# Local attention with the band mask added in the row-maximum operation of VectorE instead of in a product on TensorE

## The chip, the cores and the metric

The kernel runs on one core of one Trainium2 chip. The metric is the device time of one execution in microseconds (us); the lower the better. The core's engines are called here as in the profile: PE (TensorE, matrix products into PSUM) with PEld (its weight loads), DVE (VectorE), ACT (ScalarE), POOL (GpSimd) and SP (SyncE, which issues the DMAs).

## The reference

One layer of a diffusion backbone over 1024 latent tokens of width 1024, with 256 context tokens in front. A modulated RMSNorm feeds one input projection and from it three token mixers: local attention over a window (8 query heads, 2 key/value heads, head width 64), global attention, and a bidirectional recurrence (HGRN2). They are lifted, gated, merged and projected; a gated feed-forward block with a depthwise convolution follows. The part that the change touches is the local attention:

```
qpos = blk * BLOCK + arange(BLOCK)          # BLOCK = WINDOW = 128, 8 blocks
kpos = (blk - 1) * BLOCK + arange(3 * BLOCK)
valid = (|kpos - qpos| <= WINDOW) & (kpos >= 0) & (kpos < S)
s_loc = where(valid, q @ band(k).T * hd**-0.5, -1e30)
s_ctx = q @ ck.T * hd**-0.5                 # 256 context keys, no mask
p = softmax([s_ctx, s_loc, s_sink])         # one sink logit per head
o = p_ctx @ cv + p_loc @ band(v)
```

Each block of 128 queries thus sees the 256 context keys, and its own block of keys with the one before and the one after. In the block before, a key counts if its place is at or after the query's; in the block after, if it is at or before it. The own block has no mask. The first and last block of queries have no block before or after.

## The kernel before, in words

All products are made at near float32 precision from pairs of operands in the type float32r: a number is split into a high part and the rest (`KH` and `KL` for the keys, `ph` and `pl` for the probabilities), and the products of the parts are summed in PSUM. A query's two parts lie side by side in one operand `QT` (64 rows each), so that two products, with `KH` and with `KL`, give the scores.

The stages follow each other: modulation and context, the projections and the recurrence (to about 500 us), the token-major projections with RoPE, local attention (`br == 0`), global attention (`br == 1`), the merge, the feed-forward block. The order of the instructions on each engine comes from a planner: it takes the program in the order in which it is written, with priorities, and orders it by estimated costs. A helper `weave` sets the written order: it draws from several generators in proportion to their lengths.

In `attention`, an iteration `it` is one block of 128 queries (`tt`, 8 of them) and one key/value group (`g`, 2 of them, 4 heads each): 16 iterations. First `lead` loads all keys and values (`prep`: DMA, casts, transposes `kt`), prepares the queries of two iterations (`qprep`: DMA, split, transposes `pq`, cast `QT`) and makes the scores of iteration 0. Then each iteration weaves three things: the scores and softmax of iteration `it + 1` (`softmax_window`), the product with the values of iteration `it` (`values`), and products of the output gates as filler (`gate_unit`, tile `gz`, with weights loaded and split at lines 172 to 176 into `wr`, `wh`, `wl`).

In `softmax_window`, a head's scores `sa` are a row of 512 or 640 numbers for each of 128 queries, in one of two PSUM buffers of two banks (`mm2`, which the global attention and others also use). Lines 1387 and 1388 make the 256 context scores, 1390 and 1391 those of the band of keys (256 columns in the first and last block, 384 elsewhere). Line 1392 adds the mask: a product of the unit matrix `identr` with the needed columns of `trir`, three blocks of 128 columns that hold 0 or -1e30. Line 1395 takes the negated row maximum on DVE, line 1397 its minimum with the negated sink logit `nsnk`; line 1399 is the exponential on ACT, from PSUM into the tile `pw` (8 buffers), with the row sums as accumulated result. Lines 1404 to 1407 work out the sink's share and the reciprocal of the sum, and line 1409 scales `pw` on POOL. In `values`, line 1321 transposes `pw` (tile `pp`, four of 128x128), line 1325 casts it to `ph` on ACT, line 1326 subtracts to `pl` on DVE, and lines 1307 and 1308 multiply with the values (`po`).

The masks come as `tri`, three blocks of 128x128 in float32 (192 KB), by a DMA at line 1241 on SP's queue, ahead of the loads of the keys (line 1251), and are cast to `trir` on ACT at line 1243.

Of the kernel before, what the change touches and what calls it, by code (L numbers as in the profile page):

```python
# [9 lines left out]
F32 = mybir.dt.float32  # L10
F32R = mybir.dt.float32r
U32 = mybir.dt.uint32
AF = mybir.ActivationFunctionType
ALU = mybir.AluOpType
AX = mybir.AxisListType
# [3 lines left out]
P = 128  # L19
# [1209 lines left out]
def attention(tc, nc, ap_, br, ins, kv_d, q_d, y_d, mm2, bank, ident, identr, fill_gen, fill_steps):  # L1229
    V, A, G, T, SP = nc.vector, nc.scalar, nc.gpsimd, nc.tensor, nc.sync  # L1230

    def tl(shape, tag, nm, bufs=2, dt=F32):
        return ap_.tile(shape, dt, tag=tag, name=f"{tag}{br}_{nm}", bufs=bufs)

    NK = 10
    KH = tl([P, 2, NK * P], "KH", 0, 1, F32R)
    KL = tl([P, 2, NK * P], "KL", 0, 1, F32R)
    VHL = tl([P, NK, 2, 2, 64], "VHL", 0, 1, F32R)
    if br == 0:
        tri = tl([P, 3 * P], "tri", 0, 1, F32)  # L1240
        SP.dma_start(tri, ins["tri"])
        trir = tl([P, 3 * P], "trir", 0, 1, F32R)
        A.copy(trir, tri)
        snk = tl([P, 8], "snk", 0, 1)
        SP.dma_start(snk, ins["sink"].to_broadcast([P, 8]))
        nsnk = tl([P, 8], "nsnk", 0, 1)
        V.tensor_scalar(out=nsnk, in0=snk, scalar1=-1.0, scalar2=None, op0=ALU.mult)
# [43 lines left out]
    def scores(it):  # L1291
        tt, g = divmod(it, 2)
        QT = QTs.pop(it)
        if br == 0:
            yield from softmax_window(nc, tl, mm2, tt, g, f"{it}_", QT, KH, KL, trir, identr, snk, nsnk, res)
        else:
            yield from softmax_global(nc, tl, mm2, g, f"{it}_", QT, KH, KL, res, rs)

# [49 lines left out]
    res, rs = {}, {}  # L1348
    def lead():
        for k0 in range(0, NK, 2):  # L1350
            prep(k0)
            yield
        qprep(0)
        qprep(1)
        yield
        yield from scores(0)
# [14 lines left out]
    man.close()  # L1371


def softmax_window(nc, tl, mm2, tt, g, nm, QT, KH, KL, trir, identr, snk, nsnk, res):
    V, A, G, T = nc.vector, nc.scalar, nc.gpsimd, nc.tensor
    lo, hi = max(tt - 1, 0), min(tt + 1, LT - 1)
    kts = [0, 1] + [2 + b for b in range(lo, hi + 1)]
    nk = len(kts) * P
    w = nk - 256
    m0 = (lo - (tt - 1)) * P  # L1380
    Ps = []
    st = tl([P, 8, 4], "st", nm)
    ng, sm, sk = st[:, 0], st[:, 1], st[:, 2]
    for h in range(4):

        sc = mm2(f"sa{nm}{h}").rearrange("p a b -> p (a b)")[:, 256:256 + nk]
        T.matmul(sc[:, :256], QT[:, h], KH[:, g, :256], start=True, stop=False)
        T.matmul(sc[:, :256], QT[:, h], KL[:, g, :256], start=False, stop=True)
        k = (2 + lo) * P
        T.matmul(sc[:, 256:], QT[:, h], KH[:, g, k:k + w], start=True, stop=False)  # L1390
        T.matmul(sc[:, 256:], QT[:, h], KL[:, g, k:k + w], start=False, stop=False)
        T.matmul(sc[:, 256:], identr, trir[:, m0:m0 + w], start=False, stop=True)
        n1 = ng[:, h:h + 1]
        hs = g * 4 + h
        V.tensor_reduce(out=n1, in_=sc, axis=AX.X, op=ALU.max, negate=True)

        V.tensor_tensor(out=n1, in0=n1, in1=nsnk[:, hs:hs + 1], op=ALU.min)
        pw = tl([P, 640], "pw", f"{nm}{h}", 8)
        A.activation(pw[:, :nk], sc, AF.Exp, bias=n1, accum_out=sm[:, h:h + 1])
        Ps.append(pw)  # L1400
        if h % NB == NB - 1:
            b = slice(h - NB + 1, h + 1)
            bs = slice(hs - NB + 1, hs + 1)
            V.tensor_tensor(out=sk[:, b], in0=snk[:, bs], in1=ng[:, b], op=ALU.add)
            A.activation(sk[:, b], sk[:, b], AF.Exp)
            V.tensor_tensor(out=sm[:, b], in0=sm[:, b], in1=sk[:, b], op=ALU.add)
            V.reciprocal(sm[:, b], sm[:, b])
            for j in range(h - NB + 1, h + 1):
                G.tensor_scalar(out=Ps[j][:, :nk], in0=Ps[j][:, :nk], scalar1=sm[:, j:j + 1], scalar2=1.0,
                                op0=ALU.mult, op1=ALU.mult)  # L1410
        yield
    res[2 * tt + g] = ((lambda h, n: Ps[h][:, n * P:(n + 1) * P]), kts)
# [86 lines left out]
def _tile_w(w, nk, ncol):  # L1499

    K, N = w.shape
    return np.ascontiguousarray(w.reshape(nk, P, N // ncol, ncol).transpose(2, 1, 0, 3).reshape(N // ncol, P, nk * ncol))


def prepare(inputs):
    i = {k: np.asarray(v) for k, v in inputs.items()}
    f = np.float32
    r = {}
    r["xT"] = np.ascontiguousarray(i["x"][0].T)
    r["x"] = np.ascontiguousarray(i["x"][0])  # L1510
    r["ctxT"] = np.ascontiguousarray(i["ctx"][0].T)
    r["cc"] = np.ascontiguousarray(np.stack([i["c"][0], i["c_ctx"]], -1).reshape(KT, P, 2).transpose(1, 0, 2))
    wm = i["w_mod"][0]
    r["w_mod"] = wm
    r["w_mod01"] = np.ascontiguousarray(
        wm[:, :2 * D].reshape(KT, P, 2, KT, P).transpose(3, 1, 2, 0, 4).reshape(KT, P, 2 * KT * P))
    r["b_mod"] = np.ascontiguousarray(i["b_mod"][0].reshape(48, P).T)
    r["gains"] = np.ascontiguousarray(
        np.stack([i["norm_mix"][0], i["norm_ffn"][0], i["norm_final"]]).reshape(3, KT, P).transpose(2, 0, 1))
    r["lb"] = np.ascontiguousarray(np.stack([i["lb_fwd"][0], i["lb_bwd"][0]]).reshape(8, P).T)  # L1520
    r["gn"] = np.ascontiguousarray(i["gn_c"][0].reshape(P, 1))

    eo = np.concatenate([np.arange(0, 64, 2), np.arange(1, 64, 2)])
    r["qn"] = np.ascontiguousarray(i["qn_b"][0][eo].reshape(1, 64))
    r["kn"] = np.ascontiguousarray(i["kn_b"][0][eo].reshape(1, 64))
    r["sink"] = np.ascontiguousarray(i["sink_a"][0].reshape(1, 8))
    w = i["w_in"][0]
    sizes = (512, 128, 128, 512, 128, 128, 512, 512, 512, 512, 512, 3072)
    o = np.cumsum((0,) + sizes)
    seg = [w[:, o[j]:o[j + 1]] for j in range(12)]  # L1530
    pe = lambda m: m.reshape(D, -1, 64)[:, :, eo].reshape(D, -1)
    r["w_tm"] = np.ascontiguousarray(np.concatenate(
        [pe(seg[0]), pe(seg[1]), seg[2], pe(seg[3]), pe(seg[4]), seg[5]], 1)
        .reshape(2, 4, P, 6, 256).transpose(3, 0, 2, 1, 4).reshape(12, P, 1024))
    r["w_cm"] = _tile_w(np.concatenate([seg[6], seg[7], seg[8], seg[9], seg[10], seg[11]], 1), KT, P)
    r["w_branch"] = np.concatenate([_tile_w(i["w_branch"][0, n], 4, 256) for n in range(3)], 0)
    r["w_out"] = _tile_w(i["w_out"][0], KT, P)
    r["w_up"] = _tile_w(i["w_up"][0], KT, P)
    wd = i["w_down"][0]

    r["w_down"] = np.ascontiguousarray(
        wd.reshape(FT // 2, 2, P, 2, 512).transpose(3, 0, 2, 1, 4).reshape(FT, P, 1024))
    r["w_dlast"] = np.ascontiguousarray(
        wd.reshape(FT, P, KT, P)[:, :, 4:].transpose(2, 1, 0, 3).reshape(4, P, FT * P))
    r["conv"] = np.ascontiguousarray(
        np.concatenate([i["w_dw"][0], i["b_dw"]], 0).reshape(4, 2 * FT, P).transpose(2, 1, 0))

    r["ident"] = np.eye(P, dtype=f)
    j, t = np.meshgrid(np.arange(P) % HB, np.arange(HB), indexing="ij")
    r["hmask"] = np.ascontiguousarray(  # L1550
        np.stack([((j >> l) ^ 1) == (t >> l) for l in range(NMASK)], 1).astype(np.uint32))
    q, k = np.meshgrid(np.arange(P), np.arange(P), indexing="ij")
    z = np.zeros((P, P))
    r["tri"] = np.concatenate([np.where(k >= q, z, -1e30), z, np.where(k <= q, z, -1e30)], 1).astype(f)
    row = np.repeat(np.arange(L // 64), 64).astype(f)
    col = np.tile(np.arange(64), L // 64).astype(f)
    inv = (f(10000.0) ** (-np.arange(0, 32, 2, dtype=f) / f(32))).astype(f)
    ang = np.concatenate([row[:, None] * inv, col[:, None] * inv], -1).astype(f)
    cs = np.stack([np.cos(ang), np.sin(ang)], 1).astype(f)
    r["rope"] = np.ascontiguousarray(cs.reshape(LT, P, 2, 32).transpose(1, 0, 2, 3))  # L1560
    return r
# [15 lines left out]
```

## Time and profile before

| what | value |
|---|---|
| time, median of 3 runs | 2128.88 us (2126.53 to 2129.55) |
| span of the profiled execution | 2127.9 us |
| instructions | 30555 |
| PE busy | 2085.8 us (98%), 11686 matmuls |
| PE weight loads busy | 1743.1 us (82%) |
| DVE busy | 1380.5 us (65%) |
| ACT busy | 1001.2 us (47%) |
| POOL busy | 288.1 us (14%) |
| DMA | 229.28 MB, 108 GB/s on average |
| local attention, first to last `sa` product | 699.6 to 877.1 us |

The page gives the span from the first to the last instruction as the profiled execution's only time; the median of the runs lies 1.0 us above it. Busy times are those of the profiled execution. PE's are sums over matmuls whose ends are modelled, and neighbours overlap, so a matmul's share of the time is read from the distance of starts. In the lists of groups, a row gives the line, the engine, the operation, what is written from what, the count, then the sum and the mean (ns) of busy time, and then the idle time before it with the one that ended it.

### The profile page before, as it was taken

What the parts mean: (1) busy time and instruction counts of PE and PEld (TensorE: products, weight loads), DVE (VectorE), ACT (ScalarE), POOL (GpSimd) and SP (SyncE); (2) the same over time, 40 slices, a digit from 0 to 9 for tenths busy, and PEclk for the clock granted to TensorE, in tenths of its full rate; (3) what the DMA queues carried; (4) which work ended last, traced back from release to release, by engine and by line L of the source; (5) the groups of instructions that cost most, each with busy time, mean ns of one, the idle gap of its engine ahead of it and who ended that gap; (6) DMA issues with size and microseconds to landing.
All of it is one profiled execution on the core that took longest, in us unless ns stands there. A gap on an engine that the chain in (4) does not pass through costs nothing.

```text
span 2127.9 us, 30555 instructions
## 1 busy us (share of the span) xinstructions
PE 2085.8 (98%) x11686; PEld 1743.1 (82%) x11686; DVE 1380.5 (65%) x2299; ACT 1001.2 (47%) x1761; POOL 288.1 (14%) x257
## 2 busy tenths in 40 slices
PE   7999999999999999999999999999999999999997
PEld 4888888888988888878888788888888888888887
DVE  4736756636665777678887746569777777664423
ACT  4333333311123777678888734346445544453222
POOL 0000000010021222100000000011333344100111
PEclk9999999999999999999999999999999999999999
DMA  9511111136543211211100354641222222285342
GB/s 359 207 44 36 46 50 41 46 113 214 186 137 123 78 59 41 80 55 35 35 28 28 115 200 142 194 156 55 99 79 89 80 80 88 81 287 201 109 126 86
DMA packets 95490, 229.28 MB, mean 108 GB/s; under 512 B 10736, under 2 KB 35824, under 8 KB 94320
## 3 DMA queue, kind: packets, MB, share of 16 engines
q1 hardware_dynamic: 95344, 227.33, 32.1%
q8 instruction: 92, 1.51, 0.3%
q14 instruction: 54, 0.44, 0.1%
HBM read 181.68 MB, written 45.61 MB: 107 GB/s over the span
## 4 chain that ended last, share of the span: by engine, by line
PE 69%; DVE 3%; ACT 2%; issue 1%; DMA 1%; POOL 1%; SPq 0%; DVEq 0%; ACTq 0%; POOLq 0%
PE pp L1321 4%; PE gz L199 3%; PE dn L929 3%; PE dn L928 3%; PE dn L930 3%; PE gz L200 3%; PE gz L201 3%; PE up L852 2%; PE up L853 2%; PE up L854 2%; PE po L1307 2%; PE po L1308 2%; PE br L200 2%; PE br L201 2%; PE br L199 2%; PE upd L853 2%
## 5 line engine op out<-in xcount | busy, mean ns | idle before, releaser
L175 ACT CAST wh<-wr 128x1024 fp32r<-128x1024 f32 (+1 forms) x139 | 145.1, 1044 | 398.7 <-PE dn L929 69.1
L176 DVE TENSOR_TENSOR wl<-wr,wh 128x1024 fp32r<-128x1024 f32 (+1 forms) x139 | 171.1, 1232 | 221.1 <-ACT wh L175 206.7
L1326 DVE TENSOR_TENSOR pl<-pp,ph 128x512 fp32r<-128x512 f32 x236 | 159.3, 687 | 29.2 <-ACT ph L1325 23.5
L199 PE MATMUL gz<-hh,wh 128*128 128x512 f32 x384 | 156.3, 408 | 3.1 <-ACT gs L523 3.1
L1325 ACT CAST ph<-pp 128x512 fp32r<-128x512 f32 x236 | 135.7, 587 | 37.4 <-PE pp L1321 35.3
L201 PE MATMUL gz<-hh,wl 128*128 128x512 f32 x384 | 152.3, 397 | 0.0
L200 PE MATMUL gz<-hl,wh 128*128 128x512 f32 x384 | 152.1, 396 | 0.0
L210 PE MATMUL tm<-wl,hh 128*128 128x256 f32 x384 | 108.9, 283 | 3.3 <-DVE wl L176 3.3
L209 PE MATMUL tm<-wh,hh 128*128 128x256 f32 x384 | 108.9, 284 | 0.9 <-ACT qo L615 0.9
L211 PE MATMUL tm<-wh,hl 128*128 128x256 f32 x384 | 108.6, 283 | 0.0
L1307 PE MATMUL po<-ph,VHL 128*128 128x512 f32 x236 | 106.1, 450 | 1.4 <-ACT ph L1325 1.0
L929 PE MATMUL dn<-ac,wh 128*128 128x512 f32 x256 | 99.7, 390 | 0.0
L930 PE MATMUL dn<-ac,wl 128*128 128x512 f32 x256 | 99.6, 389 | 0.0
L928 PE MATMUL dn<-ac,wh 128*128 128x512 f32 x256 | 99.6, 390 | 0.0
L1308 PE MATMUL po<-pl,VHL 128*128 128x512 f32 x236 | 97.1, 411 | 0.1
L199 PEld LDWEIGHTS gz<-hh,wh 128*128 128x128 f32 x384 | 72.7, 189 | 17.2 <-ACT gs L523 5.2
L201 PEld LDWEIGHTS gz<-hh,wl 128*128 128x128 f32 x384 | 72.5, 189 | 15.0
L200 PEld LDWEIGHTS gz<-hl,wh 128*128 128x128 f32 x384 | 72.8, 190 | 11.6
L210 PEld LDWEIGHTS tm<-wl,hh 128*128 128x128 f32 x384 | 73.7, 192 | 4.3 <-DVE wl L176 4.0
L1321 PE MATMUL pp<-ident,plat 128*128 128x128 f32 x512 | 76.6, 273 | 0.0
L1321 PEld LDWEIGHTS pp<-ident,plat 128*128 128x128 f32 x512 | 62.7, 140 | 16.9 <-DVE pl L1326 1.2
L199 PE MATMUL br<-yh,wh 128*128 128x512 f32 x192 | 74.3, 390 | 1.6 <-ACT yh L1468 1.6
(1420 smaller groups left out, 5898.7 us busy)
## 6 DMA issues: line engine op xcount, KB each, us to landing
wr<-in_w_cm SPq DMA_DIRECT2D x48, 512.0 KB, 3.7
wr<-in_w_up SPq DMA_DIRECT2D x44, 512.0 KB, 3.5
wr<-in_w_down SPq DMA_DIRECT2D x33, 512.0 KB, 3.5
wmr<-in_w_mod SPq DMA_DIRECT2D x32, 512.0 KB, 4.5
gate_d<-gs SPq DMA_DIRECT2D x48, 256.0 KB, 2.3
sgt<-gate_d SPq DMA_DIRECT2D x24, 512.0 KB, 3.4
act_d<-u SPq DMA_DIRECT2D x22, 512.0 KB, 2.6
st<-act_d SPq DMA_DIRECT2D x44, 256.0 KB, 4.5
```

The costliest lines, as they stand in the source:

```text
L175: A.copy(hi[:, :n], raw[:, :n])
L176: (lo_eng or V).tensor_tensor(out=lo[:, :n], in0=raw[:, :n], in1=hi[:, :n].bitcast(F32), op=ALU.subtract)
L199: T.matmul(psl, wh[:, k, c], hh[:, k0 + k, cols], start=s, stop=False)
L200: T.matmul(psl, wh[:, k, c], hl[:, k0 + k, cols], start=False, stop=False)
L201: T.matmul(psl, wl[:, k, c], hh[:, k0 + k, cols], start=False, stop=e)
L210: T.matmul(psl, hh[:, k, toks], wl[:, k % 4, :], start=False, stop=False)
L928: T.matmul(z, w[0][:, c], h[0], start=s, stop=False)
L929: T.matmul(z, w[0][:, c], h[1], start=False, stop=False)
L930: T.matmul(z, w[1][:, c], h[0], start=False, stop=e)
L1307: T.matmul(po, vv, ph, start=n == 0, stop=False)
L1321: T.transpose(pp[:, h], PT(h, n), ident)
L1326: V.tensor_tensor(out=pl, in0=pp, in1=ph.bitcast(F32), op=ALU.subtract)
```

## The change

The mask product on PE goes. In place of the reduction and the minimum on DVE, one DVE operation adds the scores in PSUM and a band of masks in SBUF, multiplies by -1, writes the row to `pw`, and gives the minimum of that row and `nsnk`. The exponential then works in place on `pw` in SBUF, with scale -1. The band holds nine blocks of 128 columns, of which 640 columns from the first on serve the inner and the last block of queries (the last takes 512 of them), and the last 512 the first block; the context keys have zeros in it. It stays in float32, and the cast of the masks goes.

```diff
     if br == 0:
-        tri = tl([P, 3 * P], "tri", 0, 1, F32)
-        SP.dma_start(tri, ins["tri"])
-        trir = tl([P, 3 * P], "trir", 0, 1, F32R)
-        A.copy(trir, tri)
+        band = tl([P, 9 * P], "band", 0, 1, F32)
+        SP.dma_start(band, ins["band"])
...
-    m0 = (lo - (tt - 1)) * P
+    m0 = 0 if tt else 5 * P
...
-        T.matmul(sc[:, 256:], QT[:, h], KL[:, g, k:k + w], start=False, stop=False)
-        T.matmul(sc[:, 256:], identr, trir[:, m0:m0 + w], start=False, stop=True)
+        T.matmul(sc[:, 256:], QT[:, h], KL[:, g, k:k + w], start=False, stop=True)
         n1 = ng[:, h:h + 1]
         hs = g * 4 + h
-        V.tensor_reduce(out=n1, in_=sc, axis=AX.X, op=ALU.max, negate=True)
-
-        V.tensor_tensor(out=n1, in0=n1, in1=nsnk[:, hs:hs + 1], op=ALU.min)
         pw = tl([P, 640], "pw", f"{nm}{h}", 8)
-        A.activation(pw[:, :nk], sc, AF.Exp, bias=n1, accum_out=sm[:, h:h + 1])
+        V.tensor_tensor_reduce(out=pw[:, :nk], in0=sc, in1=band[:, m0:m0 + nk], scale=-1.0, scalar=nsnk[:, hs:hs + 1],
+                               op0=ALU.add, op1=ALU.min, accum_out=n1)
+        A.activation(pw[:, :nk], pw[:, :nk], AF.Exp, bias=n1, scale=-1.0, accum_out=sm[:, h:h + 1])
...
-    r["tri"] = np.concatenate([np.where(k >= q, z, -1e30), z, np.where(k <= q, z, -1e30)], 1).astype(f)
+    bl, br = np.where(k >= q, z, -1e30), np.where(k <= q, z, -1e30)
+    r["band"] = np.concatenate([z, z, bl, z, br, z, z, z, br], 1).astype(f)
```

More of the change, by code (lines that the diff above doesn't have):

```diff
@@ L1294, in scores @@
         if br == 0:
-            yield from softmax_window(nc, tl, mm2, tt, g, f"{it}_", QT, KH, KL, trir, identr, snk, nsnk, res)
+            yield from softmax_window(nc, tl, mm2, tt, g, f"{it}_", QT, KH, KL, band, snk, nsnk, res)
         else:
@@ L1371, in attention, with softmax_window @@
     man.close()
-def softmax_window(nc, tl, mm2, tt, g, nm, QT, KH, KL, trir, identr, snk, nsnk, res):
+def softmax_window(nc, tl, mm2, tt, g, nm, QT, KH, KL, band, snk, nsnk, res):
     V, A, G, T = nc.vector, nc.scalar, nc.gpsimd, nc.tensor
```

## The prediction

> **What bounds the kernel now.** I read the busy time by stretch first, cut where local attention lies.
>
> ```profile
> core 0: us, PE busy (x) PEld busy (x) DVE busy (x) ACT busy (x) POOL busy (x), PEclk, DMA share, GB/s
> 690.00:880.00 190.00, 188.44 (x1124) 161.62 (x1123) 146.78 (x450) 140.06 (x357) 48.95 (x64) 1.00 0.19 56
> 0.00:2128.00 2128.00, 2085.81 (x11686) 1743.08 (x11686) 1380.50 (x2299) 1001.23 (x1761) 288.14 (x257) 1.00 0.32 108
> ```
>
> The columns are the stretch, its length, then each engine's busy time. PE is busy 188.4 of 190 us in the stage of local attention, and 2085.8 of 2128 in all; DVE stands at 77% of the stage and ACT at 74%. The clock is 1.00, so no throttle has to be reckoned with. A busy PE could still hide stalls inside its modelled durations, so the second view is the waits of PE and of its weight loads in the stage:
>
> ```profile
> PE pp L1321 <- ACT QT L1288: 0.7, 4, 0.2
> ...
> PEld pp L1321 <- ACT QT L1288: 1.6, 4, 0.4
> PEld pp L1321 <- POOL pw L1409: 1.1, 4, 0.3
> ```
>
> The columns are the total, the times and the longest. The largest wait of PE is 0.7 us in 190, and its weight loads lose at most 1.6 us to any one releaser. The third view is the chain that ended last, cut to the stage:
>
> ```profile
> by line: PE pp L1321 16.5%; PE gz L199 11.0%; PE gz L200 10.8%; PE gz L201 10.2%; PE po L1307 7.9%; PE po L1308 7.9%; PE sa L1391 5.0%; PE sa L1390 5.0%; PE sa L1392 5.0%; PE sa L1387 3.9%; PE sa L1388 3.4%; ACT pw L1399 2.3%; PE pq L1286 1
> ```
>
> The mask product, line 1392, is 5.0% of 190 us of this chain, 9.5 us. So it lies on the path that sets the end, and TensorE's issue of instructions is the limit here. After the stage nothing waits for a fixed moment: the next stage is again PE work, and what ends earlier here starts earlier there.
>
> **The change part by part.** *The mask product removed (64 times, with its weight load).* Its duration in the rows, about 0.34 us, is not what it costs, since matmuls overlap. What counts is the distance between starts, from the timeline of PE:
>
> ```profile
> 753.49 0.34 PE L1390 MATMUL sa<-KH,QT 128*128 128x384 f32 x1
> 753.66 0.34 PE L1391 MATMUL sa<-KL,QT 128*128 128x384 f32 x1
> 753.84 0.34 PE L1392 MATMUL sa<-trir,identr 128*128 128x384 f32 x1
> 754.02 0.60 PE L1321 MATMUL pp<-ident,pw 128*128 128x128 f32 x4
> ...
> 873.15 0.28 PE L1392 MATMUL sa<-trir,identr 128*128 128x256 f32 x1
> 873.26 0.60 PE L1321 MATMUL pp<-ident,pw 128*128 128x128 f32 x4
> ```
>
> Three products over 384 columns take 754.02 - 753.49 = 0.53 us, 0.177 each; one over 256 takes 873.26 - 873.15 = 0.11. There are 48 of the wide form (the twelve (tile, group) pairs inside the sequence, four heads each) and 16 of the narrow one (the first and the last tile): 48 x 0.177 + 16 x 0.11 = 10.3 us. The chain says 9.5. These are the bounds; I take 10.0 us saved, between two readings of the same thing.
>
> *The DVE work.* The reduction and the small minimum go, one fused operation comes that reads the scores from PSUM and the band from SBUF, writes the whole masked row to `pw`, and gives the row minimum. The trace has no such operation; the nearest rows:
>
> ```profile
> L1395 DVE TENSOR_REDUCE st__6601<-sa 128x1 f32<-128x640 f32 x4 | 3.3, 822 | 2.3 <-PE pp L1321 1.2 <-PE sa L1392 1.1
> L1395 DVE TENSOR_REDUCE st__6194<-sa 128x1 f32<-128x512 f32 x4 | 2.7, 686 | 0.9 <-PE sa L1392 0.9
> L1326 DVE TENSOR_TENSOR pl<-pp,ph 128x512 fp32r<-128x512 f32 x72 | 49.0, 686 | 6.0 <-ACT ph L1325 5.3
> L1282 DVE SCALAR_TENSOR_TENSOR qs_q<-qf_q,qs_q 128x256 fp32r<-128x256 f32 x16 | 6.7, 418 | 4.0 <-PE sa L1392 2.2 <-ACT qs_q L1281 1.8
> 690.00:880.00 190.00, 9.89 (x64) 1.00 0.19 56
> 690.00:880.00 190.00, 50.30 (x64) 1.00 0.19 56
> ```
>
> The last two rows are the busy time of line 1397 and of line 1395 alone. `pl` has the new operation's operands (one from PSUM, one from SBUF, a full row out) and costs 686 ns for 512 elements, the same as the reduction. So the likely price is that of the reduction, 50.3 us for 64, and 9.9 us of line 1397 go: DVE 146.8 - 9.9 = 136.9 us. The low end is this; for the high end the operation runs at half the rate. The rows at 640 and 512 give (822 - 686) / 128 = 1.06 ns per element, so half rate adds 0.68 us at 640 and 0.54 at 512: 48 x 0.68 + 16 x 0.54 = 41 us, DVE 178 us. An accumulated result may need a read-out besides; ACT's costs
>
> ```profile
> L1399 ACT ACTIVATE pw<-sa,st__6457 x4: 795/800/813, 721.3 to 726.6; 128x640 f32<-128x640 f32 x4
> L1399 ACT ACTIVATION_READ_ACCUMULATOR pw<-sa,st__6457 x4: 193/197/212, 722.0 to 727.3; 128x1 f32 x4
> L1399 ACT ACTIVATE pw<-sa,st__6194 x4: 677/682/688, 703.4 to 708.3; 128x512 f32<-128x512 f32 x4
> L1443 ACT ACTIVATE pc__8872<-pc__8872,st__8871 x4: 495/498/518, 916.8 to 923.3; 128x256 f32<-128x256 f32 x4
> ```
>
> 0.2 us, so 0 to 64 x 0.2 = 13 us. I take full rate with a small read-out, DVE about 143 us beside a PE that needs 178 to 180. It is hidden by PE. The fused operation waits for the products as the reduction did, with the same work queued behind it on DVE. One wait is new to DVE: as the writer of `pw` it now waits for the transposes that last read that buffer, which ACT did before. With eight buffers these belong to the iteration before last, all issued before this one's scores, so I count nothing for it.
>
> The row that bears on half rate is line 1282: two float32 sources, both in SBUF, 256 elements in 418 ns. At 1.06 ns per element that is 271 ns and a fixed 147, so full rate, though that operation has no accumulator. [...]
>
> *The exponential* reads `pw` in SBUF instead of PSUM. From PSUM, 512 and 640 elements take 682 and 800 ns, 0.92 ns per element, so 256 would take 0.446; line 1443, in place in SBUF, takes 0.498. So +0.05 us each, 3.3 us on ACT (74% busy before). It frees the score buffer earlier, after the DVE operation; the stage waits almost nothing for that now, so I count nothing.
>
> *Where ACT's cover is thin.* At four boundaries between iterations the chain leaves PE for ACT's queue:
>
> ```profile
> 739.89 0.41 ACT wh L175
> ...
> 740.84 0.88 ACT pw L1399 x2
> ...
> 743.09 0.59 ACT QT L1288
> 743.73 0.55 PE pp L1321 x3
> ```
>
> The weight cast, an exponential, a gate copy, two copies of `ytmp` and the cast of `QT` run back to back from 739.9 to 743.7, and the transposes behind need `QT`; PE waited there, the 0.7 us in four times above. This burst doesn't shrink, while PE's work beside it loses one or two mask products, 0.18 to 0.35 us, and the exponential in it grows by 0.05. So some 0.3 us at each of four places are not gained: +1.2 us; bounds 0 and 4 x 0.7 (four products of an iteration) = 2.8.
>
> *The masks' load.* `band` is 9 blocks of 64 KB, 576 KB, where `tri` had 192; the cast `trir` goes.
>
> ```profile
> L1241 SPq DMA_DIRECT2D tri<-in_tri x1: 447/447/447, 678.8 to 678.8; - x1
> DMA to landing us min/median/max: 3.8/3.8/3.8
> ...
> 682.66 0.51 ACT L1243 CAST trir<-tri 128x384 fp32r<-128x384 f32 x1 [0.29 <-DMA tri<-in_tri]
> ...
> 685.18 0.54 PE L1270 MATMUL kt<-identr,qs_kk 128*128 128x128 f32 x4 [0.26 <-ACT qs_kk L1261]
> ...
> wr<-in_w_cm SPq DMA_DIRECT2D x48, 512.0 KB, 3.7
> ```
>
> A 512 KB load lands in 3.7 us against 3.8 for `tri`, so the size alone hardly shows, but the first keys are issued behind it on the same queue, and PE waits for them (0.26 us at 685.18). The price lies between -0.3 (that wait gone with ACT's cast) and 384 KB at the 512 / 3.7 = 138 KB per us of that load, +2.8 us, all at once. I take +0.5. The band itself has time: the first exponential, at 703.4, comes 20 us after the old cast.
>
> *Sum.* -10.0 + 1.2 + 0.5 = -8.3 us against the profiled span of 2127.9, so 2119.6. The median of the runs, 2128.88, is 1.0 us above that span, so 2120.6 us.
>
> **The rivals.** *The order eats it (no change).* The order on the engines is planned anew with other durations. Each of 16 iterations has only to lose 0.6 us more on PE for 10 us to go. For it: ACT's bursts above, and the scaling on POOL, for which weight loads already wait 1.1 us in four places and which now has a DVE beside it that writes full rows. Against it: DVE and ACT are idle a quarter of the stage and PE hardly waits. Time: 2128.9 - 10 + 16 x (0.4 to 0.7) = 2125 to 2130, say 2127.
>
> *The fused operation is slow (slower).* One mechanism: half rate on DVE. DVE then needs 178 us of work and up to 13 of read-outs, 178 to 191, in a stage where PE needs 188.4 - 10.0 = 178.4. DVE would be the bound. PE, kept in order by its own queue, is idle for 2% of the span; for DVE, fed by two engines, I assume 5%, and the stage takes 187 to 201 us instead of 190: 2126 to 2140, say 2135 with a read-out. It decides where DVE's work reaches about 180 us, that is at (180 - 86.6) / 64 = 1.46 us for each fused operation (86.6 is 146.8 without lines 1395 and 1397); below about 1.2 us nothing shows. For it: no row has this operation. Against it: lines 1326 and 1282.
>
> *The gain is larger.* The earlier release of the score buffers and a better fit of the new order take ACT's waits away: the full 10.3 us plus the 3.4 us that the rows of waits show, 2115.5.
>
> **How the numbers follow.** Forecast, 2116.5 to 2124.5: 0.57. Larger gain: 0.11. Order eats it: 0.18. Slow operation: 0.10. Some other loss in the new order beyond 0.2%: 0.04. About 0.2%, 4.3 us, is what this measurement can tell from no change; the edge of the faster class is 2124.6. Faster: 0.57 + 0.11 and a small part of the order rival's, 0.70. Same: 0.16. Slower: 0.14. The range reaches from the larger gain, with a bit of room, 2114, through the whole of the order rival, 2130; the slow operation lies outside.
>
> **What would show it.** Right: line 1392 gone from PE with 64 fewer products; the fused operation at about 0.82 to 0.95 us for 640 elements; the stage from the first `sa` product to the last some 8 to 10 us shorter with PE still above 97% busy; the exponential at 0.84 to 0.85 us. Wrong: a fused operation above 1.2 us with PE waiting for ACT's exponential or POOL's scaling behind it; PE's idle time in the stage above 8 us; or a start of local attention delayed by over 2 us, with the keys' load as its cause.

## The result, and the profile after

The changed kernel takes 2119.15 us (median of 4 runs, 2117.39 to 2122.27) against 2127.70 us for the kernel before in the same series (2126.43 to 2129.55). The ratio is 0.9959, 95% interval 0.9944 to 0.9973: faster by 8.6 us, where 8.3 had been forecast. A repeat with another series of the kernel before gave 2119.38 against 2129.49 us, ratio 0.9956 (0.9943 to 0.9970).

The profile of the changed kernel, first the busy times of its engines over the whole, then the stage of local attention by stretch (columns as before; the stage is cut at 872 us, since it ends earlier):

```profile
PE 2078.3 (98%) x11622; PEld 1735.2 (82%) x11622; DVE 1379.4 (65%) x2299; ACT 1003.0 (47%) x1760; POOL 289.7 (14%) x257
...
690.00:872.00 182.00, 178.94 (x1062) 150.98 (x1061) 144.52 (x451) 143.35 (x360) 49.83 (x64) 1.00 0.19 60
```

There are 64 matmuls fewer (11622 for 11686) and one ACT cast fewer. DVE's count stays at 2299, since the 64 minima that went are replaced by 64 read-outs of an accumulator.

The groups of the changed kernel by shape, for the fused operation and for the exponential:

```profile
L1393 DVE CUSTOM_DVE_ANT_0 pw<-sa,band,nsnk 128x640 f32<-128x640 f32 x48 | 42.2, 880 | 5.5 <-PE sa L1389 4.9
...
L1393 DVE CUSTOM_DVE_ANT_0 pw<-sa,band,nsnk 128x512 f32<-128x512 f32 x16 | 11.9, 747 | 2.9 <-PE sa L1389 1.9 <-PE pp L1319 0.8
...
L1395 ACT ACTIVATE pw<-pw,st__8062 128x640 f32<-128x640 f32 x4 | 3.3, 834 | 0.0
```

The fused operation takes 880 ns for 640 elements, 58 ns more than the reduction took, and 1.04 ns per element from one shape to the other, where the reduction took 1.06: the reduction's rate, which the prediction calls full. The exponential from SBUF takes 0.83 us where it took 0.80. In the timeline of DVE the read-out is a row of its own, and the next operation starts with it:

```profile
729.12 0.88 DVE L1393 CUSTOM_DVE_ANT_0 pw<-sa,band,nsnk 128x640 f32<-128x640 f32 x1
729.93 0.08 DVE L1393 DVE_READ_ACCUMULATOR2_ANT st__6575<- 128x1 f32 x1
729.93 0.69 DVE L1324 TENSOR_TENSOR pl<-pp,ph 128x512 fp32r<-128x512 f32 x1
```

So the read-out costs the queue nothing here (the subtraction starts at 729.93 as well). The waits of PE and of its weight loads in the stage:

```profile
PE pp L1319 <- POOL pw L1405: 1.5, 5, 0.6
PE pq L1284 <- DVE qs_q L1280: 1.4, 1, 1.4
...
PEld pp L1319 <- POOL pw L1405: 3.5, 8, 0.9
...
PEld pp L1319 <- ACT QT L1286: 1.6, 4, 0.4
```

The weight loads' wait for `QT` is what it was, 1.6 us; PE's own, 0.7 us before, is not in the list any more. New is the wait of the transposes `pp` for the scaling on POOL, 3.5 us of the loads where it was 1.1 and 1.5 us of PE, and the wait for the second queries (`pq`) grew from 0.5 to 1.4 us.

**A cleaner measure than the time.** Executions of one kernel differ by several microseconds (the four of the changed kernel by 4.9), and part of this lies ahead of the change (5.4 us between two executions of the same work, in the last section). So the experiments are read by a stretch as well, from the start of the last token-major product (`tm`) to the first key transpose of the global attention (`kt`). It holds all of local attention, and the same PE work in every kernel but for what the experiment takes out. Before:

```profile
663.90:894.56 230.66, 227.61 (x1313) 193.00 (x1312) 167.05 (x495) 156.47 (x390) 51.65 (x66) 1.00 0.23 72
```

The changed kernel:

```profile
663.70:885.96 222.26, 217.87 (x1250) 182.46 (x1249) 164.71 (x495) 158.60 (x389) 51.84 (x66) 1.00 0.24 76
```

The stretch is 8.4 us shorter, and PE's busy time in it falls by 9.7 us. The repeat of the changed kernel:

```profile
664.00:884.60 220.60, 217.64 (x1249) 182.37 (x1248) 164.50 (x495) 158.22 (x389) 51.51 (x66) 1.00 0.25 77
```

There the stretch was 220.6 us, 10.1 shorter, so differences under 2 us in it aren't read. Of every other kernel one execution was profiled. What follows the stretch takes 1231.6 us after and 1233.3 before, much the same: the gain is made in this stage.

### The profile page after: what moved, and what is told of

The parts are those of the page before. It is cut to its first block, busy times and chain, and to the rows that moved or that the text cites. A ratio compares the mean times of both kernels' runs of the same rounds, so it can differ in the third digit from the quotient of the medians.

```text
span 2117.6 us, 30402 instructions
## 1 busy us (share of the span) xinstructions
PE 2078.3 (98%) x11622; PEld 1735.2 (82%) x11622; DVE 1379.4 (65%) x2299; ACT 1003.0 (47%) x1760; POOL 289.7 (14%) x257
## 4 chain that ended last, share of the span: by engine, by line
PE 69%; DVE 3%; ACT 2%; issue 1%; POOL 1%; DMA 1%; DVEq 0%; ACTq 0%; POOLq 0%; SPq 0%
PE pp L1319 5%; PE gz L199 3%; PE gz L200 3%; PE gz L201 3%; PE dn L929 3%; PE dn L930 3%; PE dn L928 3%; PE up L852 2%; PE up L853 2%; PE up L854 2%; PE po L1305 2%; PE po L1306 2%; PE br L200 2%; PE br L201 2%; PE br L199 2%; PE upc L854 2%
## 5 line engine op out<-in xcount | busy, mean ns | idle before, releaser
L733 ACT ACTIVATE u<-c,cw 128x1024 f32<-128x1024 f32 x38 | 47.3, 1246 | 61.9 <-DVE c L889 33.1
```

## The experiments

The theory ahead of the runs was that the 64 slots taken from PE are the gain. The rival was that the gain comes from the other half of the change, a shorter path on DVE and score buffers that are freed earlier.

**The product alone removed.**

```diff
-        T.matmul(sc[:, 256:], QT[:, h], KL[:, g, k:k + w], start=False, stop=False)
-        T.matmul(sc[:, 256:], identr, trir[:, m0:m0 + w], start=False, stop=True)
+        T.matmul(sc[:, 256:], QT[:, h], KL[:, g, k:k + w], start=False, stop=True)
```

(on the kernel before)

> The kernel before with the mask product alone taken from PE; reduction, minimum and exponential stay as they were, and the mask is left out of the computation. Theory (the gain is the 64 slots of the product on PE): 9.5 to 10.3 us less than before, less up to 1.2 us at ACT's bursts, so a ratio of 0.9952 to 0.9960 and a time some 0 to 1.5 us below the changed kernel's, which pays for the longer load. Rival (the gain comes from the one DVE operation in place of two and the score buffer freed earlier): a ratio of 0.9985 to 1.000.

Measured: 2123.49 us against 2128.91, ratio 0.9977 (0.9968 to 0.9986). By this time it fits neither. The nine runs had a higher clock than the 27 of before, though, 0.9976 against 0.9964 in the mean. With each run's span multiplied by its granted clock, the 5.4 us become 2.9, as an estimate, which is the rival's edge. The stretch, at a clock of 1.00 like before's, says the same:

```profile
660.30:888.20 227.90, 221.45 (x1250) 180.68 (x1249) 172.62 (x495) 155.46 (x390) 51.97 (x66) 1.00 0.23 73
```

It is only 2.8 us shorter than before. The waits of this kernel, in a window around local attention, show where the slots went:

```profile
PE pp L1321 <- POOL pw L1408: 2.5, 4, 0.9
PE po L1307 <- ACT ph L1325: 1.6, 4, 0.8
...
PEld pp L1321 <- POOL pw L1408: 8.8, 20, 1.2
PEld sa L1387 <- ACT pw L1398: 3.7, 14, 0.4
PEld po L1307 <- ACT ph L1325: 3.1, 4, 1.0
```

With the product gone and the softmax's path as it was, the weight loads of the transposes wait 8.8 us in 20 places for the scaling of the probabilities, 3.7 us in 14 for a score buffer that the exponential still reads. Before, these two were 1.1 and 0.5:

```profile
PEld sa L1387 <- ACT pw L1399: 0.5, 2, 0.3
```

So the reading is that PE was the bound with next to no margin: the path from the scores to the scaled probabilities was almost as long. The next runs test it.

**The product kept, the rest of the change made.**

```diff
+        trir = tl([P, 3 * P], "trir", 0, 1, F32R)
+        A.copy(trir, band[:, 2 * P:5 * P])
...
-        T.matmul(sc[:, 256:], QT[:, h], KL[:, g, k:k + w], start=False, stop=True)
+        T.matmul(sc[:, 256:], QT[:, h], KL[:, g, k:k + w], start=False, stop=False)
+        c0 = (lo - (tt - 1)) * P
+        T.matmul(sc[:, 256:], identr, trir[:, c0:c0 + w], start=False, stop=True)
```

(on the changed kernel)

> The changed kernel with the mask product put back on PE beside the fused operation (the mask is added twice). Theory: the 10 us come back, and with the longer load of the masks and the cast that follows it the time is 0 to 2 us above before, a ratio of 1.000 to 1.001. Rival (gain from DVE's shorter path and the buffers): a ratio of 0.996 to 0.998.

Measured: 2126.10 us, ratio 0.9990 (0.9981 to 0.9999). The stretch:

```profile
662.60:893.10 230.50, 226.55 (x1313) 192.96 (x1312) 166.00 (x495) 160.99 (x390) 52.66 (x66) 1.00 0.23 74
```

It is the same as before, so the fused operation by itself gains nothing in its stage. The 2.8 us of the medians lie outside it or in the spread of the runs; this stays open. The two halves of the change give 2.8 and 0.2 us of the stretch apart, and 8.4 to 10.1 together. The medians alone would not show this, since 5.4 and 2.8 us make 8.2; with the spans multiplied by the clock they are, as an estimate, 2.9 and 1.6 us apart and 9.5 together (the repeat).

**Is it the score buffers?** Against the changed kernel the exponential reads PSUM again, so that the buffer is held as long as before, while DVE's path stays short:

```diff
-        A.activation(pw[:, :nk], pw[:, :nk], AF.Exp, bias=n1, scale=-1.0, accum_out=sm[:, h:h + 1])
+        A.activation(pw[:, :nk], sc, AF.Exp, bias=n1, accum_out=sm[:, h:h + 1])
...
-    r["band"] = np.concatenate([z, z, bl, z, br, z, z, z, br], 1).astype(f)
+    r["band"] = np.concatenate([z, z, z, z, z, z, z, z, z], 1).astype(f)
```

> The changed kernel with the exponential reading the scores from PSUM again instead of the row that the fused operation wrote, so that a score buffer is held until the exponential is done; the masks are zeros here, so the mask is left out of the computation (same operations, same load). Measured by the stretch on PE from the last token-major product to the first key transpose of the global attention (before 230.7 us, changed kernel 222.3 and 220.6, product alone removed 227.9). Theory B (the early release of the score buffers is what lets PE use the freed slots): 225 to 228 us, a ratio of 0.9968 to 0.9985. Theory C (it is the shorter path on DVE, one operation instead of two, to the exponential and POOL's scaling): 220 to 223 us, a ratio of 0.9945 to 0.9965.

Measured: 2120.81 us, ratio 0.9965 (0.9953 to 0.9978). The stretch:

```profile
663.70:887.50 223.80, 218.44 (x1249) 182.93 (x1248) 165.22 (x495) 156.68 (x389) 51.57 (x66) 1.00 0.24 76
```

It is 1.5 to 3.2 us more than the changed kernel's and 4.1 less than with the product alone removed. Its weight loads do wait for the buffer again, though less:

```profile
PEld pp L1319 <- POOL pw L1405: 4.1, 9, 0.6
...
PEld sa L1385 <- ACT pw L1395: 1.5, 4, 0.4
```

The stretch lies between the two theories' numbers, nearer to C's, and the ratio at the edge of C's. So the buffers are the smaller part at most.

**Is it the path to the scaling?** Against the run with the product alone removed, the scaling on POOL is gone:

```diff
-            for j in range(h - NB + 1, h + 1):
-                G.tensor_scalar(out=Ps[j][:, :nk], in0=Ps[j][:, :nk], scalar1=sm[:, j:j + 1], scalar2=1.0,
-                                op0=ALU.mult, op1=ALU.mult)
```

> The kernel before without the mask product, as in the run of the product alone removed, and without the scaling on POOL: the probabilities stay unscaled, and the mask is left out too. There PE's weight loads waited 8.8 us in 20 places for the scaling and 3.7 us in 14 for a score buffer. Theory C (the path to POOL's scaling eats the slots): the stretch falls from 227.9 to 219 to 223 us, a ratio of 0.994 to 0.996. Theory B (the buffers): it stays at 225 to 228 us, and the waits for the buffer stay at 3 us or more.

Measured: 2117.08 us, ratio 0.9943 (0.9929 to 0.9956), and the stretch:

```profile
665.90:884.55 218.65, 216.72 (x1249) 181.67 (x1248) 166.12 (x495) 154.75 (x390) 2.01 (x2) 1.00 0.24 76
```

It is 218.65 us, 9.2 less than with the scaling, although the loads still wait for the score buffer:

```profile
PEld sa L1387 <- ACT pw L1398: 4.1, 13, 0.4
```

Theory C's numbers are met (the stretch came out 0.35 us below its range), and B's sign, 4.1 us of waits for the buffer, turns out to cost little of the stretch. The gain comes from behind the exponential: the mean distance from the reduction's start to the exponential's is 1.95 us in both kernels, and DVE's reduction takes 0.82 us in both, so it is not that DVE gets ahead faster without POOL. The wait for the scaled probabilities is what ate the freed slots. With the scaling this run also takes away the wait for the sink's share and the reciprocal that the scaling needs, and these two aren't separated.

**How long may DVE's step be?** Ahead of the fused operation stands an unused reduction of 256 scores, then of the whole row:

```diff
+        V.tensor_reduce(out=st[:, 3, h:h + 1], in_=sc[:, :256], axis=AX.X, op=ALU.max)
         V.tensor_tensor_reduce(out=pw[:, :nk], in0=sc, ...
```

> The changed kernel with a second, unused reduction of 256 scores per head on DVE ahead of the fused operation, about 0.41 us by line 1395's rows, which makes the step as a whole 1.29 us and DVE's work in the stage 144.5 + 26 = 171 us beside some 178 of PE. Theory (PE is the bound until DVE's work reaches about 180 us, a step of 1.46 us): 0 to 3 us above the changed kernel, still below before, a ratio of 0.996 to 0.9975. Rival (DVE's path matters at any length): 26 us of work show at half or more, a ratio above 1.001.

> The same with an unused reduction of the whole row, 0.69 to 0.82 us, which makes the step 1.43 to 1.70 us and DVE's work in the stage 144.5 + 50.3 = 195 us. Theory: DVE becomes the bound, the stage takes 195 / 0.95 = 205 us instead of 182, so 13 to 25 us above the changed kernel, a ratio of 1.002 to 1.008 against before. Rival (the work still hides, since the planner moves DVE's work of the stage about): a ratio below 0.999.

Measured: 2124.40 us, ratio 0.9983 (0.9975 to 0.9991), and 2147.41 us, ratio 1.0086 (1.0073 to 1.0100). The stretches of the two, in this order:

```profile
665.20:892.53 227.33, 221.09 (x1250) 183.89 (x1248) 185.85 (x559) 159.77 (x389) 54.51 (x66) 0.99 0.24 75
```

```profile
664.00:915.32 251.32, 230.52 (x1254) 184.29 (x1253) 206.77 (x559) 159.35 (x389) 53.79 (x66) 0.97 0.21 68
```

Both came out dearer than expected: the small dose adds 5.1 to 6.7 us to the stretch, the large one 29 to 31. Part of this is the clock, 0.99 and 0.97 here (0.9925 and 0.9728 by the trace's records) where the changed kernel had 1.00. As an estimate, that is 1.7 and 6.8 us; it leaves 3.4 to 5.0 us for the small dose, still above what was expected, and 22 to 24 for the large one, within it. In the small dose PE is busy 2.14 us of the five from 875 us on, and the clock is 0.72 in the five after them; that the one brings the other isn't shown.

DVE is busy 82% of both stretches, but these begin some 35 us ahead of the scores. While the iterations run it is much fuller; the changed kernel, the small and the large dose:

```profile
700.00:865.00 165.00, 161.99 (x961) 136.89 (x961) 134.23 (x420) 130.23 (x326) 47.04 (x60) 1.00 0.18 55
```

```profile
700.00:875.00 175.00, 171.65 (x1008) 144.08 (x1007) 160.41 (x504) 136.45 (x341) 50.22 (x63) 1.00 0.18 54
```

```profile
700.00:875.00 175.00, 160.29 (x912) 127.53 (x910) 162.91 (x451) 123.97 (x308) 44.36 (x56) 1.00 0.14 45
```

That is 81%, 92% and 93%. In the large dose DVE is close to being the bound: the scores wait for it, 2.86 us in the mean from the start of the last score product to that of DVE's step, where the changed kernel has 0.79. In the small dose this distance is 1.01 us, and the waits of PE show where the rest was lost:

```profile
PE pp L1319 <- POOL pw L1406: 4.3, 9, 1.6
...
PEld pp L1319 <- POOL pw L1406: 10.1, 19, 1.9
```

0.42 us more ahead of the exponential reach the scaling, and the weight loads of the transposes wait for it again, 10.1 us. So a longer step costs time by that path before DVE has none left. How much of the 0.42 us came through directly, and how much by a DVE that is 92% busy and so comes later to everything, isn't separated.

**The load of the band behind the keys; the sink's share on ACT.**

```diff
-        SP.dma_start(band, ins["band"])
...
         qprep(0)
         qprep(1)
+        if br == 0:
+            SP.dma_start(band, ins["band"])
```

> The changed kernel with the load of the band issued behind the loads of the keys and of the first queries instead of ahead of them. Theory (the 576 KB ahead of the keys delay the start of local attention; in the changed kernel PE waited 1.36 us for the second queries, and the first score product came 0.7 us later than before): 1 to 2 us below the changed kernel. Rival (the load hides, what waited was the order): no difference, within 0.5 us; if the band comes too late for the first fused operation, PE waits there instead and it is slower.

```diff
-            V.tensor_tensor(out=sk[:, b], in0=snk[:, bs], in1=ng[:, b], op=ALU.add)
-            A.activation(sk[:, b], sk[:, b], AF.Exp)
+            A.activation(sk[:, b], ng[:, b], AF.Exp, bias=snk[:, bs])
```

> The changed kernel with the sum of sink logit and row minimum made as the bias of ACT's small exponential instead of in a DVE operation of its own, 64 fewer small DVE operations (0.15 us each) and a shorter chain to the scaling on POOL. Theory (the rest of the lost gain is the waits of PE and its weight loads for POOL's scaling and ACT's burst, 1.5 and 3.5 us in the changed kernel's stage): the waits shrink a little, 0.5 to 2 us below the changed kernel. Rival (PE's slots are all that counts): within 0.5 us.

> Both, the late load of the band and the sink in ACT's bias. Theory: their gains add, 1.5 to 3.5 us below the changed kernel, a ratio of 0.9935 to 0.9955 against before. Rival: within 1 us of the changed kernel.

Measured in one series with the changed kernel (2119.38 us, ratio 0.9956): 2117.80 us and 0.9951 (0.9938 to 0.9963) with the late load, 2118.63 us and 0.9951 (0.9938 to 0.9963) with the sink in the bias, 2119.78 us and 0.9953 (0.9939 to 0.9966) with both. The stretches are 223.5, 222.1 and 222.0 us. None is told apart from the changed kernel; the gains that were expected aren't shown. (The late load's stretch has a clock of 0.99, worth an estimated 1.7 us, so it too is the changed kernel's.) With the late load PE waited 1.7 us for the first keys instead of 1.4 for the queries. With the sink in the bias the waits for POOL grew, though one DVE operation of the path was gone:

```profile
PE pp L1319 <- POOL pw L1404: 3.5, 7, 0.7
...
PEld pp L1319 <- POOL pw L1404: 5.9, 9, 0.9
```

So the count of operations on the path doesn't settle the wait alone. POOL's scaling itself was slower there, 0.89 us for 640 numbers in the mean where the changed kernel has 0.80 to 0.81; why was not tried. Whether the rest is the planned order wasn't tried here; the next run changes that order.

**Scores earlier in the iteration.** If the transposes of iteration `it + 1` wait for the scaling of its last heads, their scores should be made sooner:

```diff
-        weave((scores(it + 1), S_LEN * (4 + br)) if it + 1 < n_it else (None, 0),
+        weave((scores(it + 1), (S_LEN if br else 1.8) * (4 + br)) if it + 1 < n_it else (None, 0),
```

> The changed kernel with the four score steps of local attention woven earlier into each iteration (the length by which they are drawn against the others is 1.8 x 4 instead of 1.35 x 4; global attention as it was). If what is left of the loss is the wait for POOL's scaling of the last heads (1.5 us of PE, 3.5 us of its weight loads in the changed kernel), that wait goes and the stretch is 1 to 3 us shorter than the changed kernel's, a ratio of 0.9935 to 0.9955. Rival (the order is balanced, and scores drawn early only crowd DVE and ACT): 0 to 3 us longer.

Measured: 2114.97 us against 2128.53, ratio 0.9939 (0.9926 to 0.9951), the fastest of all here that compute the whole. The stretch and its waits:

```profile
664.60:881.89 217.29, 215.85 (x1252) 182.48 (x1250) 163.76 (x495) 157.24 (x389) 51.97 (x66) 1.00 0.25 78
```

```profile
PE pp L1319 <- POOL pw L1405: 0.6, 1, 0.6
...
PEld pp L1319 <- POOL pw L1405: 1.2, 2, 0.9
```

The wait for POOL falls from 3.5 to 1.2 us, and the stretch by 3.3 to 5.0 us. This kernel wasn't in one series with the changed kernel, and the two intervals against before overlap; the stretch, of one profiled execution, is what tells them apart.

**The fused operation with two sources in SBUF.**

```diff
+        for r in range(4):
+            V.tensor_tensor_reduce(out=tjn, in0=band[:, :640], in1=band[:, 512:1152], scale=-1.0, scalar=nsnk[:, r:r + 1],
+                                   op0=ALU.add, op1=ALU.min, accum_out=tja[:, r:r + 1])
+            V.tensor_tensor(out=tjn, in0=band[:, :640], in1=band[:, 512:1152], op=ALU.add)
```

> The changed kernel with four fused operations more on two SBUF sources of 640 float32 each, with accumulated minimum, and four plain sums of the same sources, at the start of local attention. [...]

```profile
L1249 DVE CUSTOM_DVE_ANT_0 tj<-band,nsnk x4: 877/877/885, 684.8 to 691.2; 128x640 f32<-128x640 f32 x4
L1251 DVE TENSOR_TENSOR tj<-band x4: 818/818/826, 685.7 to 692.3; 128x640 f32<-128x640 f32 x4
```

The fused operation takes 877 ns, where with one source in PSUM it took 880, and the plain sum of the same two sources takes 818. At half rate, the high end that the prediction reckoned with, it would be 0.68 us more, an estimated 1.56. So with both sources in SBUF this operation keeps its rate.

## Why the prediction was right, point by point

- *The slots of the mask product, -10.0 us.* About right in size: put back beside the fused operation, the product made the stretch 8.2 to 9.9 us longer. (PE's busy time is a poorer measure: with the same 64 products gone it fell by 9.7 us in the changed kernel and by 6.2 with the product alone removed.) But the argument that PE's issue alone is the limit was too strong. The same product removed alone gave 2.8 us of the stretch. The slots count only with the softmax's path shortened as well. The prediction left that out: it had DVE's step hidden by PE, and said of the score buffers "I count nothing".
- *The softmax's path, not priced.* By the rows of starts, the mean distance from the reduction's start to the exponential's start over 64 heads was 1.78 us before, 1.95 with the product alone removed and 1.18 in the changed kernel. So the change shortened this part by 0.6 us a head. Not all of it reaches the end: from the exponential's start to the scaling's it is 2.24, 2.20 and 2.65 us, and the whole path, from the start of a head's last product into its scores (before, the mask product) to the end of the scaling, is 5.42, 5.76 and 5.40. The change thus keeps the path from growing when the product goes, 0.36 us a head, rather than making it shorter than before. How much of this is the operation saved and how much the order on DVE isn't separated, and the mean alone doesn't set the wait: with the sink in the bias it was 5.30 us, and the loads waited 5.9.
- *The fused operation at full rate, hidden.* Right: 0.88 us, read-out 0.08 us and free, within the 0.82 to 0.95 named. DVE's work in the stage, 144.5 us up to 872, was put at 143.
- *The rival of the slow operation.* It was rightly held unlikely. Half rate, from which its 178 us of DVE work came, is shown by no run: the fused operation took 0.88 us for 640 elements, with its first source in PSUM or in SBUF. What would follow from a DVE with that much work, the large dose shows, with DVE 93% busy and scores that wait for it. But its turning point was put too late: "below about 1.2 us nothing shows" and a decision at 1.46 us came from DVE's total time. At 1.29 us (the small dose) 5 to 7 us of the stretch were lost already, 3.4 to 5.0 without the drop of the clock, much of it by the wait of the transposes for POOL.
- *ACT's burst, +1.2 us.* The wrong place. The loads' wait for `QT` stayed at 1.6 us, and PE's own went. A loss of this size was there, at the scaling on POOL: 1.5 us of PE, and weight loads that wait 3.5 us for 1.1. This is the wait that the rival of the order had named.
- *The band's load, +0.5 us.* The load landed in 5.2 us where `tri` took 3.8. Moved behind the keys it changed nothing that can be told apart, so this term is neither shown nor refuted; it is under 2 us.
- *The buffers' earlier release, 0.* Small, but likely not nothing: held again, the stretch is 1.5 to 3.2 us longer, where differences under 2 aren't read.

The sum came out right for a reason that is partly luck: the missed dependence worked in the change's favour, because both halves were made together, and a loss of the size that was put at ACT's burst turned up at POOL.

## What to carry to other kernels

A full engine with almost no waits isn't yet a bound with room below it: other paths may be only little shorter, and the first thing that a removed instruction buys may be a wait for the next of them. Here the product alone removed took the weight loads' wait for the scaling from 1.1 to 8.8 us, and the stretch fell by 2.8 us where 10.0 had been counted. Before counting slots as gain, take the distance from the last producer to the first consumer around the work that shrinks, here scores to scaled probabilities as a whole and not one part of it, and compare it with the time that the full engine gives it. Where such a wait appears, moving the producer earlier in the written order (3 to 5 us of the stretch here, by one number) can be worth a good part of what removing work is. And a share of busy time is taken over the part in which the work runs: with its idle ends, DVE's 92% read as 82%.

## What the runs showed that was not expected

- The two halves of the change don't add: 2.8 and 0.2 us of the stretch apart, 8.4 to 10.1 together.
- An execution's time varies before the change begins. Up to the last token-major product PE ran 4512 matmuls in the changed kernel with the sink in the bias and as many in the one with the late load:

```profile
0.00:665.70 665.70, 644.83 (x4512) 549.07 (x4513) 395.38 (x757) 189.36 (x311) 55.17 (x53) 0.99 0.36 122
```

```profile
0.00:660.30 660.30, 641.01 (x4512) 546.67 (x4513) 395.32 (x757) 189.40 (x311) 55.23 (x53) 1.00 0.36 123
```

  5.4 us apart, as much as the effects that were looked for. The first execution has two places at half clock in this part, 3.41 us long each by the trace's records, the second none:

```profile
492.00:495.40 3.40, 3.40 (x10) 2.63 (x9) 2.14 (x2) 0.00 (x0) 0.00 (x0) 0.50 0.93 270
601.20:604.60 3.40, 3.40 (x10) 2.62 (x9) 0.00 (x0) 0.00 (x0) 0.00 (x0) 0.50 0.42 162
```

  With PE busy throughout, they cost an estimated 3.4 of the 5.4 us. What brings them, and where the rest comes from, was not tried.
